# Four low-rank intermediates of the second stream: places of their own, and their stores in GpSimd's queue

## The chip, the cores and the metric

The kernel runs on one core of one Trainium2 chip. The metric is the device time of one launch in microseconds; for the kernel before it is 1659.32 us, the median of three runs (1658.92 to 1660.64). One more execution was taken with the hardware profiler, and every row of the profile comes from that one.

Engine names in the rows: PE is TensorE (matmul), PEld its weight load, DVE is VectorE, ACT is ScalarE, POOL is GpSimd, SPq is the queue of SyncE, which here only issues DMAs. A number such as L591 is a line of the kernel.

## The reference

Two inputs, `x_prompt` and `x_sample`, each 512 tokens by 1024 in fp32, pass through the same two layers with the same weights. The kernel calls them stream 0 and stream 1. Layer 0 is a bidirectional RWKV-7 time mixing, layer 1 a gated neighbourhood attention; the change touches layer 0 only:

```
x_prev, x_next = xn shifted by one token either way
xx = 0.5 * (x_prev + x_next) - xn
lerp(j) = xn + xx * mu[j]
r, k, v = lerp(0) @ w_r, lerp(1) @ w_k, lerp(2) @ w_v ;  z = xn @ w_z
for d in (0, 1):                       # forward and backward scan
    w_log = -softplus(-(w0[d] + tanh(lerp(3+d) @ w1[d]) @ w2[d])) - 0.5
    a     = sigmoid(a0[d] + (lerp(5+d) @ a1[d]) @ a2[d])
    ...                                # decay, scan over 512 tokens, bonus
```

`w1` and `a1` project from 1024 to 64, `w2` and `a2` from 64 back to 1024. So each stream has four low-rank intermediates of 64 x 512: `tanh(lerp(3) @ w1[0])`, `tanh(lerp(4) @ w1[1])`, `lerp(5) @ a1[0]` and `lerp(6) @ a1[1]`. In the kernel they are numbered q = 0 to 3.

## The kernel before

Activations lie transposed, features on the 128 partitions and 512 tokens along the row. A 1024-wide operand is eight tiles of 128 x 512, and an fp32 product is made of three matmuls of a high and a low part: ScalarE casts the high part (L743 for weights, `whi`), VectorE subtracts it for the low part (L745, `wlo`), TensorE multiplies (L824 to L826).

The program has three stages.

The prelude (`prelude(s)`) normalizes each stream, forms the shifted differences, and accumulates the four low-rank projections of all eight tiles in PSUM. At its end, for each pair q2 of intermediates, ScalarE copies a partial sum from PSUM (L581, `lm`), VectorE combines it with its neighbours (L582, L584) and with the other partial sum (L589) into `y`, the first half of a tile `lr`; then ScalarE makes two 64 x 512 intermediates from the halves of `y` (L591, Tanh for q below 2, a copy otherwise). For stream 0 they are split into high and low parts at once and stay in SBUF. For stream 1 they go to DRAM (`save("hid", ...)`, rows `dhid<-lr`) and come back when the scan reaches that stream, near 550 us. The tile `lr` has one buffer. In the kernel before, all four intermediates of a stream are written to the same place, the first 64 partitions of the second half of `lr`.

The scan stage (`scan_phase`) follows. For a pair of heads, `prep` loads `rb` (the inverse norms, from `drn`), `k`, the low-rank weights `w2` and `r` through SyncE's queue in this order; VectorE makes `kk` in the place of `rb` (L876), ScalarE casts the weights' high part `w2h` (L878), VectorE makes the low part `w2l` (L880), ScalarE scales `kk` (L883, `km`), and TensorE multiplies the intermediates with `w2h` and `w2l` (L894, L895). Between these run the columns of the large projections (L824 to L826), with weights loaded in pieces of 128 x 512 through SyncE (`raw`) into three buffers, ScalarE's copies of finished columns (L655) and, where the planner foresees an idle TensorE, filler matmuls (L1641). After a pair's scan, `finish` loads `bv`, `ks`, `sz`; the framework may issue the load of `sz` earlier.

The last stage (`rest`) is the attention layer.

What sets the order: in the scan stage a planner in the kernel (`weave`, with a clock of modelled costs that starts at zero there) writes out the order on TensorE, VectorE and ScalarE by hand. Everything else, the prelude, the last stage and the queues of SyncE and GpSimd throughout, is put in order by the framework from priorities and a modelled timeline of its own, and the tail of the prelude is interleaved with the head of the scan stage. Each queue runs strictly in order on the chip: an instruction that waits holds all behind it.

Memory: the prelude's tiles (`xn`, `lr`, `lm`, `lw`, `xx`, `ls`) lie in a pool that is closed at its end; two pools of the scan stage are opened over the same bytes. A new tile waits for those who still use the old tiles under it, no more. In the kernel before, `rb`, `k`, `r` lie over old `xn` slots; the two `MT` tiles, cleared by GpSimd (L1672), lie over `lr` and `lm` among others; the four slots of `ls`, which the prelude uses for operands and mixed inputs, lie under `ks`, `bv`, `sz` and two small tiles of `finish`.

`save` picks the queue of a store by `store(kind)`: SyncE in the prelude; in the scan stage and later (`self.away`) GpSimd, but for three kinds.

Of the kernel before, what the change touches and what calls it, by code (L numbers as in the profile page):

```python
# [11 lines left out]
F32 = mybir.dt.float32  # L12
# [7 lines left out]
P = 128  # L20
T = 512
# [210 lines left out]
class Trunk:  # L232
# [94 lines left out]
        self.store(kind).dma_start(d, src)  # L327

    def store(self, kind):
        return self.nc.gpsimd if self.away and kind not in ("y", "x1", "h") else self.nc.sync  # L330

    def load(self, dst, src):
        self.nc.sync.dma_start(dst, src)
# [168 lines left out]
    def prelude(self, s):  # L502
        nc = self.nc
        vt, gps, act = nc.vector, nc.gpsimd, nc.scalar
        xs = []
        if s == 0:
            self.vectors()
        for k in range(KT):
            if s == 0 and k == self.WFIRST:
                self.first = [self.weight(self.a["w_z"][0])]  # L510
            t = self.t("xn", (P, T + 2), 16, F32, self.lp)
            self.load(t[:, 1:T + 1], self.a["x"][s][k * P:(k + 1) * P, :])
            xs.append(t)
            if s == 0:

                lo, hi = self.pair()
                act.activation(hi, t[:, 1:T + 1], AF.Identity, scale=self.vec("pre0", k))
                vt.scalar_tensor_tensor(lo, t[:, 1:T + 1], self.vec("pre0", k), hi.bitcast(F32), op0=ALU.mult, op1=ALU.subtract)
                self.xz.append((hi, lo))
                yield  # L520
        if s == 0:
            self.consts()
        acc = self.t("acc") if s else self.t("vs", bufs=self.NVS)
        for k, t in enumerate(xs):
            gps.memset(t[:, 0:1], 0.0)
            gps.memset(t[:, T + 1:T + 2], 0.0)
            self.sumsq(acc, t[:, 1:T + 1], k, vt if s or k % 2 else vt)
            yield
        rstd = self.rstd(acc)
        if s == 0:  # L530
            self.rstd0 = rstd
        yield
        xn, xx = [], []
        for k, t in enumerate(xs):
            x = t[:, 1:T + 1]
            vt.scalar_tensor_tensor(x, x, self.vec("pre0", k), rstd, op0=ALU.mult, op1=ALU.mult)
            xn.append(x)
            yield
        if s == 0:
            yield from self.lora_weights()  # L540
        for k, t in enumerate(xs):
            u = self.t("xx", (P, T), 16, F32, self.lp)
            vt.tensor_tensor(u, t[:, 2:T + 2], t[:, 0:T], op=ALU.add)
            xx.append(u)
            yield
        self.shift[s] = xn, xx

        def mixed(kind, j, k):

            t = self.t("ls", (P, T), 4, F32, self.lp)  # L550
            self.lerp(t, xn[k], xx[k], 8 * j + k)
            self.save("l" + kind, s, k, t)

        pm = self.p("pf", (P, 2, T))
        ps = (self.p("pm"), self.p("us"))
        for k in range(KT):
            if s == 0:
                hi, lo = self.xz[k]
            else:
                hi, lo = (self.t("ls", (P, T), 4, F32R, self.lp) for _ in range(2))  # L560
                self.halves(xn[k], lo, hi, self.alt(k))
            for q2 in range(2):
                for out, w in ((pm[:, q2], self.wm), (ps[q2], self.wl)):
                    a, b = (m[:, k % 4] for m in w[2 * q2 + k // 4])
                    nc.tensor.matmul(out, a, hi, start=(k == 0), stop=False)
                    nc.tensor.matmul(out, a, lo, start=False, stop=False)
                    nc.tensor.matmul(out, b, hi, start=False, stop=(k == KT - 1))
                yield
            for kind, j in (("k", 1), ("r", 0), ("v", 2)) if s else ():
                mixed(kind, j, k)  # L570
                yield
        for q2 in range(2):
            mw = self.t("lm", (P, KT * P), 1, F32, self.lp)[:, 0:T + 2]
            lr = self.t("lr", (P, KT * P), 1, F32, self.lp)
            y, u = lr[:, 0:T], lr[0:64, T:2 * T]
            gps.memset(mw[:, 0:1], 0.0)
            gps.memset(mw[:, T + 1:T + 2], 0.0)
            if s == 0:
                vt.tensor_tensor(mw[:, 1:T + 1], pm[:, q2], rstd, op=ALU.mult)
            else:  # L580
                act.copy(mw[:, 1:T + 1], pm[:, q2])  # L581
            vt.tensor_tensor(y, mw[:, 2:T + 2], mw[:, 0:T], op=ALU.add)  # L582
            yield
            vt.scalar_tensor_tensor(mw[:, 1:T + 1], y, 0.5, mw[:, 1:T + 1], op0=ALU.mult, op1=ALU.subtract)  # L584
            if s == 0:
                vt.tensor_tensor(y, ps[q2], rstd, op=ALU.mult)
                vt.tensor_tensor(y, y, mw[:, 1:T + 1], op=ALU.add)
            else:
                vt.tensor_tensor(y, ps[q2], mw[:, 1:T + 1], op=ALU.add)  # L589
            for q in (2 * q2, 2 * q2 + 1):  # L590
                act.activation(u, y[64 * (q % 2):64 * (q % 2) + 64], AF.Tanh if q < 2 else AF.Copy)  # L591
                if s == 0:
                    self.hidden(q, u)
                else:
                    self.save("hid", s, q, u)
            yield
        if s == 0:
            for k in range(KT):
                mixed("v", 2, k)
                yield  # L600
        if s == 1:
            for k in range(KT):
                self.save("lz", s, k, xn[k])
# [1326 lines left out]
```

## Time and profile before

| | before |
|---|---|
| median of 3 runs | 1659.32 us (1658.92 to 1660.64) |
| the profiled execution | 1659.26 us, span 1657.5 us |
| granted TensorE clock, mean | 0.975 |
| PE busy | 1557.6 us, 94% of the span |
| DVE busy | 1217.3 us, 73% |
| ACT busy | 1013.8 us, 61% |
| POOL busy | 175.8 us, 11% |
| moved by DMA | 336.29 MB, 203 GB/s on average |

How to read the rows that follow. A row of the timeline gives the start in us from the start of the span, the busy time, the engine, the line, the operation, the tile written and the tiles read, a count, and in brackets the idle time of the engine just before it with what ended that. A DMA row on SPq or POOL is the issue alone; the data land later. A row of the waits gives who waited, for whom, the total in us, how often, and the longest. Matmuls overlap, so TensorE's busy time is not its throughput; the distance from one start to the next is the better measure.

### The profile page before, as it was taken

Reading aid. Unit: us, or ns where it says so; the run is one execution under the profiler, and the core shown is the slowest. Engines: PE = TensorE matmul, PEld = TensorE weight load, DVE = VectorE, ACT = ScalarE, POOL = GpSimd, SP = SyncE. Lnnn points to the kernel's source line nnn. Section 1 sums busy time; section 2 is a strip of 40 time slices with the busy share of each in tenths; the row PEclk is TensorE's granted clock in tenths of the full one; section 3 lists DMA queues with packets and bytes.
Section 4 is the critical chain, followed back from the end, with each engine's and each line's share of the span. In section 5 each row is a group of like instructions: output and inputs, shape, how many; then the busy total and the mean of one; then the engine's idle time right before and its main releaser. Section 6 shows DMA issues by size and latency. Waiting matters only on the chain.

```text
span 1657.5 us, 46539 instructions
## 1 busy us (share of the span) xinstructions
PE 1557.6 (94%) x18826; PEld 1197.0 (72%) x18826; DVE 1217.3 (73%) x2711; ACT 1013.8 (61%) x2027; POOL 175.8 (11%) x334
## 2 busy tenths in 40 slices
PE   7989798898999998998988999999999999999998
PEld 6867566776667776776666777777777788777776
DVE  8886469688789787897788897855577585665564
ACT  6567565766755677665575665454567665455562
POOL 0000113311101223010000011000000002100000
PEclk9989899999999999999987999999999999999999
DMA  6455578676687687675776675553765346745553
GB/s 212 154 177 180 163 247 282 211 248 214 228 263 238 209 264 249 207 252 171 243 233 227 201 251 168 178 188 126 265 224 174 109 140 205 246 158 175 171 164 103
DMA packets 176312, 336.29 MB, mean 203 GB/s; under 512 B 20928, under 2 KB 53824, under 8 KB 176096
## 3 DMA queue, kind: packets, MB, share of 16 engines
q1 hardware_dynamic: 152800, 253.60, 48.0%
q0 software_dynamic: 23296, 79.71, 13.6%
q8 instruction: 148, 2.42, 0.6%
q14 instruction: 68, 0.56, 0.1%
HBM read 227.71 MB, written 105.51 MB: 201 GB/s over the span
## 4 chain that ended last, share of the span: by engine, by line
PE 47%; DVE 8%; ACT 5%; DMA 4%; issue 3%; SPq 0%; POOL 0%; DVEq 0%; ACTq 0%; POOLq 0%
PE pg L430 6%; PE pg L431 6%; PE pg L432 6%; PE pm L824 4%; PE pm L825 3%; PE pm L826 3%; PE pf L1112 2%; PE sc L1450 2%; PE po L1483 2%; PE pt L1468 2%; PE us L1231 1%; PE zy L1184 1%; PE us L1211 1%; PE zy L1235 1%; DMA raw<-in_w_in_dram 1%
## 5 line engine op out<-in xcount | busy, mean ns | idle before, releaser
L824 PE MATMUL pm<-act,whi 128*128 128x512 f32 x640 | 285.0, 445 | 8.1 <-ACT act L793 3.2
L825 PE MATMUL pm<-act,whi 128*128 128x512 f32 x640 | 258.0, 403 | 11.7 <-DVE act L771 6.5
L826 PE MATMUL pm<-act,wlo 128*128 128x512 f32 x640 | 256.4, 401 | 5.3 <-DVE wlo L745 5.3
L824 PEld LDWEIGHTS pm<-act,whi 128*128 128x128 f32 x640 | 122.8, 192 | 51.1 <-issue 10.8
L430 PE MATMUL pg<-act,whi 128*128 128x512 f32 x384 | 158.6, 413 | 0.4 <-DVE tmp L1406 0.4
L379 ACT CAST whi<-raw 128x512 fp32r<-128x512 f32 x148 | 91.3, 617 | 106.5 <-PE pg L431 68.7
L431 PE MATMUL pg<-act,whi 128*128 128x512 f32 x384 | 152.6, 397 | 0.0
L432 PE MATMUL pg<-act,wlo 128*128 128x512 f32 x384 | 152.6, 397 | 0.0
L825 PEld LDWEIGHTS pm<-act,whi 128*128 128x128 f32 x640 | 123.5, 193 | 37.9 <-DVE act L771 16.8
L826 PEld LDWEIGHTS pm<-act,wlo 128*128 128x128 f32 x640 | 123.2, 192 | 35.0 <-DVE wlo L745 8.2
L380 DVE TENSOR_TENSOR wlo<-raw,whi 128x512 fp32r<-128x512 f32 x148 | 101.4, 687 | 60.9 <-ACT whi L379 60.2
L745 DVE TENSOR_TENSOR wlo<-raw,whi 128x512 fp32r<-128x512 f32 x160 | 109.1, 684 | 36.4 <-ACT whi L743 36.2
L743 ACT CAST whi<-raw 128x512 fp32r<-128x512 f32 x160 | 97.8, 617 | 42.0 <-PE pm L825 24.3
L430 PEld LDWEIGHTS pg<-act,whi 128*128 128x128 f32 x384 | 72.3, 188 | 15.6 <-issue 3.3
L432 PEld LDWEIGHTS pg<-act,wlo 128*128 128x128 f32 x384 | 72.2, 188 | 14.8 <-issue 0.3
L431 PEld LDWEIGHTS pg<-act,whi 128*128 128x128 f32 x384 | 72.5, 189 | 14.0 <-issue 2.5
L1016 DVE TENSOR_TENSOR etmp<-N 128x30 f32<-128x30 f32 (+14 forms) x240 | 78.6, 328 | 4.3
L1018 DVE TENSOR_TENSOR N<-etmp,N 128x30 f32<-128x30 f32 (+14 forms) x240 | 78.7, 328 | 4.0
L1461 DVE CUSTOM_DVE_ANT_0 sb<-sc,bias 128x256 f32<-128x256 f32 x128 | 49.2, 419 | 27.7 <-PE pt L1468 21.5
L1464 ACT ACTIVATE sb<-sb,mx 128x256 f32<-128x256 f32 x128 | 64.0, 502 | 6.9 <-DVE mx L1463 6.7
L1112 PE MATMUL pf<-cab 64*64 64x128 f32 (+1 forms) x2048 | 66.8, 267 | 0.5 <-issue 0.5
L1135 DVE TENSOR_TENSOR AK<-zy,cc 128x256 f32<-128x256 f32 x63 | 26.6, 422 | 52.0 <-PE zy L1090 51.9
(407 smaller groups left out, 3680.5 us busy)
## 6 DMA issues: line engine op xcount, KB each, us to landing
dab<-ab POOLq DMA_DIRECT2D x32, 1024.0 KB, 7.1
cab<-dab SPq DMA_DIRECT2D x64, 512.0 KB, 4.6
raw<-in_w_in_dram SPq DMA_DIRECT2D x128, 256.0 KB, 3.0
bias<-in_rpb_dram SPq DMA_DIRECT2D x32, 384.0 KB, 5.2
raw<-in_w_z_dram SPq DMA_DIRECT2D x32, 256.0 KB, 3.2
raw<-in_w_k_dram SPq DMA_DIRECT2D x32, 256.0 KB, 3.7
raw<-in_w_r_dram SPq DMA_DIRECT2D x32, 256.0 KB, 3.6
k<-dk SPq DMA_DIRECT2D x32, 256.0 KB, 3.6
```

Source lines behind the costliest of these rows:

```text
L379: self.nc.scalar.copy(hi, src)
L380: (eng or self.nc.vector).tensor_tensor(lo, src, hi.bitcast(F32), op=ALU.subtract)
L430: nc.tensor.matmul(ps, hi, x[k][0], start=(k == 0), stop=False)
L431: nc.tensor.matmul(ps, hi, x[k][1], start=False, stop=False)
L432: self.mm = nc.tensor.matmul(ps, lo, x[k][0], start=False, stop=(k == KT - 1))
L743: nc.scalar.copy(hi, raw[h])
L745: nc.vector.tensor_tensor(lo, raw.pop(h), hi.bitcast(F32), op=ALU.subtract)
L824: nc.tensor.matmul(ps, hi[:, at], xh, start=(k == 0), stop=False)
L825: nc.tensor.matmul(ps, hi[:, at], xl, start=False, stop=False)
L826: nc.tensor.matmul(ps, lo[:, at], xh, start=False, stop=(k == KT - 1))
L1018: vt.tensor_tensor(N[:, q + 1:, :q], tv, N[:, q + 1:, :q], op=ALU.add)
L1112: end = nc.tensor.matmul(st.f[half(a), h, 0, d, g] if st.last else st.f[half(a), h, :, d, g], ab[half(h), d, g, 2 * e[d] + 1 - a], rt if s ...
```

## The change

For stream 1, each of the four intermediates is written to a fresh tile of the tag `ls` (four slots, shared with the prelude's earlier use), instead of the one place in `lr`. The store of each, kind `hid`, is issued from GpSimd's queue instead of SyncE's. Stream 0 is as it was. Nothing else is edited; the arithmetic is the same.

```
     def store(self, kind):
-        return self.nc.gpsimd if self.away and kind not in ("y", "x1", "h") else self.nc.sync
+        return self.nc.gpsimd if kind == "hid" or self.away and kind not in ("y", "x1", "h") else self.nc.sync
...
             for q in (2 * q2, 2 * q2 + 1):
+                if s:
+                    u = self.t("ls", (P, T), 4, F32, self.lp)[0:64]
                 act.activation(u, y[64 * (q % 2):64 * (q % 2) + 64], AF.Tanh if q < 2 else AF.Copy)
                 if s == 0:
                     self.hidden(q, u)
```

More of the change, by code (lines that the diff above doesn't have):

```diff
@@ L329, in store @@
     def store(self, kind):
-        return self.nc.gpsimd if self.away and kind not in ("y", "x1", "h") else self.nc.sync
+        return self.nc.gpsimd if kind == "hid" or self.away and kind not in ("y", "x1", "h") else self.nc.sync
     def load(self, dst, src):
@@ L590, in prelude @@
             for q in (2 * q2, 2 * q2 + 1):
+                if s:
+                    u = self.t("ls", (P, T), 4, F32, self.lp)[0:64]
                 act.activation(u, y[64 * (q % 2):64 * (q % 2) + 64], AF.Tanh if q < 2 else AF.Copy)
```

## The prediction

> **What bounds the kernel now.** I read the page first, for the engine that fills the span, then the windows around the place where the change acts, then the waits, and last the timeline of each queue there. The page says that TensorE is the engine to watch:
>
> ```profile
> PE 1557.6 (94%) x18826; PEld 1197.0 (72%) x18826; DVE 1217.3 (73%) x2711; ACT 1013.8 (61%) x2027; POOL 175.8 (11%) x334
> ```
>
> TensorE's order is fixed in its queue, so an idle stretch in it that shrinks should bring the end nearer, unless a later wait eats the gain. The four intermediates are made near 173 to 186 us. The windows there (each row: the stretch, its length, busy time and count of PE, PEld, DVE, ACT, POOL, the granted clock, DMA share, GB/s):
>
> ```profile
> 170.00:182.00 12.00, 11.82 (x52) 9.16 (x51) 4.26 (x9) 5.15 (x9) 0.79 (x3) 1.00 0.56 159
> 182.00:192.00 10.00, 1.43 (x5) 0.52 (x3) 1.35 (x2) 3.49 (x10) 4.13 (x4) 0.67 0.48 157
> 192.00:200.00 8.00, 8.00 (x28) 6.53 (x29) 6.08 (x9) 5.62 (x10) 0.11 (x1) 0.77 0.16 39
> ```
>
> TensorE is full before 182 and after 192, and nearly empty between: 8.57 us of 10 idle, and every other engine mostly idle as well. This is the largest hole near the change. What ended it (engine, line, waited for: us in total, times, longest):
>
> ```profile
> DVE rb L876 <- DMA k<-dk: 8.8, 1, 8.8
> PE pm L895 <- DVE w2l L880: 4.3, 1, 4.3
> ACT lr L591 <- DMA dhid<-lr: 3.9, 2, 2.0
> ```
>
> TensorE at L895 waits for VectorE's `w2l` (L880), which stands behind `kk` (L876, writing into `rb`), and that waited 8.8 us for the load of `k`. So the question is why `k` came so late. SyncE's own waits and its queue in order of time answer it:
>
> ```profile
> SPq L327 <- ACT lr L591: 2.5, 1, 2.5
> ```
>
> ```profile
> 173.72 0.54 SPq L327 DMA_DIRECT2D dhid<-lr  x1
> 174.34 0.53 SPq L333 DMA_DIRECT2D drn<-tmp  x1
> 176.82 0.47 SPq L327 DMA_DIRECT2D dhid<-lr  x1
> ...
> 178.66 0.33 SPq L333 DMA_DIRECT2D raw<-in_w_r_dram  x1
> 182.12 3.43 SPq L327 DMA_DIRECT2D dhid<-lr  x2
> 185.66 1.18 SPq L333 DMA_DIRECT2D rb<-drn  x2
> 186.89 0.58 SPq L333 DMA_DIRECT2D k<-dk  x1
> ...
> 187.99 0.43 SPq L333 DMA_DIRECT2D sz<-dz  x1
> ...
> 193.18 5.82 SPq L333 DMA_DIRECT2D raw<-in_w_r_dram  x2
> ```
>
> After the weight load at 178.66 SyncE issues nothing until 182.12, is held between the third and the fourth `dhid` store, and only then sends the loads of `rb` and `k`. The inputs of these loads are old: the store `drn` went out at 174.34, `dk` earlier. They wait in line, not for data. ScalarE shows why the stores are late:
>
> ```profile
> 173.59 0.56 ACT L581 COPY lm<-pf 128x512 f32<-128x512 f32 x1
> 176.16 0.63 ACT L591 ACTIVATE lr<-lr 64x512 f32<-64x512 f32 x1 [2.00 <-DMA dhid<-lr]
> 176.70 0.56 ACT L655 COPY tmp<-pm 128x512 f32<-128x512 f32 x1
> 177.29 0.62 ACT L743 CAST whi<-raw 128x512 fp32r<-128x512 f32 x1
> ...
> 182.00 0.56 ACT L655 COPY tmp<-pm 128x512 f32<-128x512 f32 x1
> 184.45 0.63 ACT L591 ACTIVATE lr<-lr 64x512 f32<-64x512 f32 x1 [1.89 <-DMA dhid<-lr]
> 185.10 1.01 ACT L1670 COPY cab<-cc 64x64 f32<-64x64 f32 x4
> 186.13 0.62 ACT L878 CAST w2h<-tmp 128x512 fp32r<-128x512 f32 x1
> ```
>
> Two of the four L591 write a place that the store before them still reads, and wait 2.00 and 1.89 us for it to land.
>
> **The change part by part.** *Own places.* Each L591 of the second stream writes an own slot of `ls`. Both waits go. The second L591 runs behind L581, at about 174.2, 2.0 us earlier. Next on ScalarE is L655, which needs TensorE's first column:
>
> ```profile
> 174.67 0.39 PE L826 MATMUL pm<-act,wlo 128*128 128x512 f32 x1
> 180.86 0.39 PE L826 MATMUL pm<-act,wlo 128*128 128x512 f32 x1
> 181.09 1.46 PE L1641 MATMUL zy<-cc 128*128 128x256 f32 x6
> 186.80 0.80 PE L894 MATMUL pm<-h,w2h 128*128 128x512 f32 x1 [4.26 <-ACT w2h L878]
> 191.91 0.80 PE L895 MATMUL pm<-h,w2l 128*128 128x512 f32 x1 [4.31 <-DVE w2l L880]
> ...
> 194.21 0.63 PE L824 MATMUL pm<-act,whi 128*128 128x512 f32 x1
> ```
>
> That column ends at 174.67 + 0.39 = 175.1, so L655 moves from 176.70 to 175.1, and the cast L743 behind it by the same 1.6 us. VectorE follows:
>
> ```profile
> 177.94 0.69 DVE L745 TENSOR_TENSOR wlo<-raw,whi 128x512 fp32r<-128x512 f32 x1 [5.38 <-ACT whi L743]
> 179.17 0.69 DVE L582 TENSOR_TENSOR lr<-lm 128x512 f32<-128x512 f32 x1 [0.54 <-DMA dhid<-lr]
> ...
> 190.50 0.75 DVE L876 SCALAR_TENSOR_TENSOR rb<-k,cv,rb 128x512 f32<-128x512 f32 x1 [8.85 <-DMA k<-dk]
> 191.17 0.68 DVE L880 TENSOR_TENSOR w2l<-tmp,w2h 128x512 fp32r<-128x512 f32 x1
> ```
>
> L745 goes from 177.94 to about 176.3, and the weight load that it releases on SyncE from 178.66 to about 177.0. L582 no longer waits for a landing (0.54). With L582 at 177 and two more operations of 0.69 us, the third and fourth L591 run at about 179.1 and 179.7 without a gap, where the fourth ran at 184.45.
>
> *GpSimd's queue.* SyncE loses four issues, about 0.5 us each by the two single ones (0.54, 0.47), and with them the hold from 179.0 to 185.6. Its next item is then `rb`. If the weight load in front keeps its time, `rb` goes out at 178.66 + 0.33 = 179.0; if it moves with L745, at 177.4. From the issue of `rb` to the start of L876 the old trace has 190.50 - 185.66 = 4.84 us, with the two `rb` loads, the issue of `k` and its landing in it. So L876 starts between 182.2 and 183.8: a shift of 8.3 to 6.7 us. I take the middle, 7.5, since both ends rest on rows equally near.
>
> Is anything else late next? `w2h` (L878) stands behind the second L655 (182.00) on ScalarE; the four copies at 185.10, 1.01 us together, fall into the idle time ahead of it or behind it. TensorE's second column loses some 0.4 us of stalls, so L655 ends near 182.2 and `w2h` between 182.8 and 183.8: about as early as L876 ends (182.95 to 184.55). With `w2h` at its earliest and `k` no obstacle, L880 would start near 182.8 instead of 191.17: 8.4 us is the most that the shift can be, since TensorE's and ScalarE's own work fills the time up to there. TensorE has its six filler matmuls (1.46) until about 182.2. From L880 on, L895, `km`, the next weight cast and the third column at 194.21 follow at their old distances.
>
> *The clock.* After the hole TensorE is slow: 28 matmuls in 8.00 us (0.286 each) at a granted 0.77, against 52 in 12 us (0.231 each) at 1.00 before it. At the faster pace the 28 need 6.5 us, 1.5 less. The hole in the forecast has two pieces of about 1 to 2 us, in place of two of over 4. I cannot see from here how short a hole must be to leave the clock alone, so the gain lies between 0 and 1.5; I take 1.0, nearer to the upper end because a piece shrinks to less than half. [...]
>
> *What is added.* GpSimd takes four issues. Its queue and the landing of its stores now (the last line is min/median/max of the 64 `dvt` stores):
>
> ```profile
> 182.88 0.54 POOL L327 DMA_DIRECT2D dr<-tmp  x1 [4.64 <-ACT tmp L655]
> 187.48 3.54 POOL L1672 MEMSET MT<- 128x2048 f32 x2 [4.06 <-DMA dhid<-lr]
> ...
> DMA to landing us min/median/max: 2.4/4.7/9.6
> ```
>
> Four times 0.54 is 2.2 us on an engine 11% busy, which was idle 4.64 and 4.06 us before these two items. The memsets wait for the place of `lr`; they may now start near 180.3, so the second `dr` store could stand behind them until 183.9, 1.0 later than now; its reader is the load of `r` for the next preparation. In order behind the waiting `hid` stores stand these `dr` stores and the memsets, nobody that TensorE needs before the third column. The new places are taken over later by `sz`, `bv` and other tiles of the scan's end; the load of `sz` (187.99) is the first. It now waits for a GpSimd store: issued near 180.3, landed by 185.0 at the median, while the weight load behind `sz` would be wanted at 193.18 - 7.5 = 185.7. I cost it at nothing; without that cover (9.6 us landing) it is 189.9, 4.2 us late.
>
> **The sum.** 7.5 + 1.0 = 8.5 us earlier from the third column on. The profiled execution took 1659.26 us (span 1657.5), practically the median of the runs, 1659.32; the forecast is 1650.8. Edges of this case: 6.7 with nothing for the clock gives 1652.6, and 8.4 + 1.5 gives 1649.4.
>
> **The rivals.** *SyncE's order is held anyway, and only issue time is saved.* If the loads of `rb` and `k` hang on the end of the low-rank work and not on the queue, all that SyncE gains is four issues, 2.0 us: 1657.3. For it: the loads are into places of the pool opened behind that work. Against it: the waits list has no wait of those loads, and SyncE goes from `dhid` to `rb` in about 0.1 us. [...]
>
> *The `sz` load holds the weights.* As worked out, a landing of 9.6 us would take 4.2 of the 8.5 back: 1655.0. Against it: the median, and weights already in hand for the third column.
>
> *Slower: a load on SyncE waits for a GpSimd store, ahead of `rb` and `k`.* SyncE's and GpSimd's orders are laid by the framework from a modelled timeline. If it puts `sz` before `rb`, and on GpSimd the last `hid` store behind the memsets and the `dr` store (182.88 + 0.54 + 3.54 = 187.0), the store lands at 187.5 + 4.7 = 192.2, `rb` goes out at 192.7 instead of 185.66, and everything is 7.0 us later: 1666.3. It decides once `rb` is issued after 185.66 + 3.3 = 189.0. Against it: `sz` stands behind `rb`, `k` and `r` today, and ScalarE makes the fourth `hid` before the place of `lr` is free for the memsets.
>
> A different kind of disturbance is the last part, where the framework lays all engines' order anew:
>
> ```profile
> 1000.00:1658.00 658.00, 642.15 (x5794) 502.71 (x5792) 417.24 (x1183) 362.29 (x786) 42.76 (x76) 0.99 0.54 173
> ```
>
> Only 15.9 us of these 658 are idle on TensorE, so there is little to win and a few us to lose; this widens the range and makes no case of its own.
>
> **How the numbers follow.** The forecast has 0.66, its own range 1648.5 to 1653.5. The `sz` rival has 0.09, issue time alone 0.13, slower 0.12. A measurement here tells about 0.2%, 3.3 us, from no change: faster means below 1656.0. Forecast and `sz` make 0.75 faster, issue time 0.13 the same, 0.12 slower. The range must leave out no more than 0.2: from 1647.5, a little below the most that the shift and clock allow, up to 1658.0, which takes in `sz` and the issue-time case and leaves out the slower one.
>
> **What would show it.** Right, if no L591 of the second stream waits for `dhid`; SyncE sends `rb` before 180; L876 starts at 182 to 184 and L895 at 183 to 186; and the stretch up to 200 has the granted clock near 1. Wrong, if SyncE stands still between the weight load and `rb`, if `sz` waits and the weight load behind it comes after 187, or if L895 is early and the end is not: then the gain went into a later wait, to be looked for where TensorE idles before 1000.

## The result, and the profile after

The changed kernel takes 1652.84 us (median of 12 runs, 1647.92 to 1658.72), the kernel before beside it 1659.69 us (12 runs, 1654.07 to 1662.74). The ratio is 0.9967, 95% interval 0.9951 to 0.9982: faster by 5.5 us, between 3.0 and 8.1 (the two medians alone lie 6.9 apart). The profiled execution took 1656.04 us, its span is 1654.2 us; it lies 3 us above the median. Two lines were added, so what was L591 is L593 here, L743 is L745, L876 is L878, L895 is L897, and so on.

The same three stretches as before (columns as there):

```profile
170.00:182.00 12.00, 10.98 (x48) 8.48 (x47) 6.75 (x8) 7.33 (x15) 6.43 (x8) 1.00 0.69 188
182.00:192.00 10.00, 6.69 (x27) 4.42 (x25) 6.02 (x9) 5.61 (x11) 0.67 (x2) 1.00 0.38 135
192.00:200.00 8.00, 7.61 (x93) 6.03 (x94) 4.64 (x7) 6.61 (x15) 1.46 (x2) 1.00 0.69 213
```

Of the 8.57 us that TensorE stood still between 182 and 192, 3.31 are left, and the clock stays at 1.00. SyncE's queue:

```profile
171.32 0.33 SPq L333 DMA_DIRECT2D drn<-tmp  x1
...
178.58 0.33 SPq L333 DMA_DIRECT2D raw<-in_w_r_dram  x1
179.01 1.31 SPq L333 DMA_DIRECT2D rb<-drn  x2
180.37 0.58 SPq L333 DMA_DIRECT2D k<-dk  x1
...
181.53 0.36 SPq L333 DMA_DIRECT2D sz<-dz  x1
187.17 10.59 SPq L333 DMA_DIRECT2D raw<-in_w_r_dram  x4
```

The loads of `rb` and `k` go out at 179.01 and 180.37 instead of 185.66 and 186.89, directly behind the weight load. ScalarE and GpSimd, in order of time:

```profile
171.80 1.28 ACT L593 ACTIVATE ls<-lr 64x512 f32<-64x512 f32 x2
...
175.90 1.28 ACT L593 ACTIVATE ls<-lr 64x512 f32<-64x512 f32 x2 [1.08 <-DVE lr L589]
177.21 0.62 ACT L745 CAST whi<-raw 128x512 fp32r<-128x512 f32 x1
...
181.87 0.62 ACT L880 CAST w2h<-tmp 128x512 fp32r<-128x512 f32 x1
```

```profile
172.73 1.20 POOL L327 DMA_DIRECT2D dhid<-ls  x2 [3.53 <-ACT ls L593]
...
176.83 1.20 POOL L327 DMA_DIRECT2D dhid<-ls  x2 [1.16 <-ACT ls L593]
178.01 3.57 POOL L1674 MEMSET MT<- 128x2048 f32 x2
```

The four L593 come in two pairs, none waits for a landing, and their stores follow within a microsecond. VectorE and TensorE:

```profile
177.86 0.69 DVE L747 TENSOR_TENSOR wlo<-raw,whi 128x512 fp32r<-128x512 f32 x1 [1.99 <-ACT whi L745]
178.47 3.32 DVE L1664 COPY mrx<-cc 128x128 f32<-128x128 f32 x2
184.49 0.75 DVE L878 SCALAR_TENSOR_TENSOR rb<-k,cv,rb 128x512 f32<-128x512 f32 x1 [2.70 <-DMA k<-dk]
185.16 0.69 DVE L882 TENSOR_TENSOR w2l<-tmp,w2h 128x512 fp32r<-128x512 f32 x1
```

```profile
164.53 0.39 PE L567 MATMUL us<-ls,lw 128*128 128x512 f32 x1
...
182.54 0.50 PE L896 MATMUL pm<-h,w2h 128*128 128x512 f32 x1
185.90 0.50 PE L897 MATMUL pm<-h,w2l 128*128 128x512 f32 x1 [2.87 <-DVE w2l L882]
...
187.13 0.39 PE L826 MATMUL pm<-act,whi 128*128 128x512 f32 x1
```

The hole that is left is one wait of 2.87 us at L897, and behind it stands `k` again: VectorE's L878 waited 2.70 us for it.

Two executions differ by up to 2 us before they reach this place (in the nine profiles the last matmul of the prelude starts between 164.53 and 166.41). So below I measure from the last matmul of the prelude (L567, 164.53 here) to the first matmul with `w2l` (L897, 185.90): 21.37 us. In the kernel before:

```profile
165.45 0.39 PE L567 MATMUL us<-ls,lw 128*128 128x512 f32 x1
```

191.91 - 165.45 is 26.46 us, so 5.09 us were won at this place by these two profiles.

### The profile page after: what moved, and what is told of

Same layout as the page of the kernel before. It is cut to its first block, busy times and chain, and to the rows that moved or that the text cites. A ratio compares the mean times of both kernels' runs of the same rounds, so it can differ in the third digit from the quotient of the medians.

```text
span 1654.2 us, 46534 instructions
## 1 busy us (share of the span) xinstructions
PE 1558.4 (94%) x18826; PEld 1195.2 (72%) x18826; DVE 1220.0 (74%) x2711; ACT 1014.5 (61%) x2027; POOL 178.2 (11%) x338
## 4 chain that ended last, share of the span: by engine, by line
PE 48%; DVE 7%; ACT 5%; DMA 3%; issue 3%; POOL 0%; SPq 0%; DVEq 0%; ACTq 0%; POOLq 0%
PE pg L430 6%; PE pg L431 6%; PE pg L432 6%; PE pm L826 4%; PE pm L827 3%; PE pm L828 3%; PE pf L1114 2%; PE sc L1452 2%; PE po L1485 2%; PE pt L1470 2%; PE us L1233 1%; PE zy L1186 1%; PE us L1213 1%; PE zy L1237 1%; DMA v<-dv 1%
## 5 line engine op out<-in xcount | busy, mean ns | idle before, releaser
L747 DVE TENSOR_TENSOR wlo<-raw,whi 128x512 fp32r<-128x512 f32 x160 | 108.9, 683 | 33.3 <-ACT whi L745 33.1
L745 ACT CAST whi<-raw 128x512 fp32r<-128x512 f32 x160 | 97.8, 617 | 44.6 <-PE pm L827 23.3
```

The source lines that it names most:

```text
L745: nc.scalar.copy(hi, raw[h])
L747: nc.vector.tensor_tensor(lo, raw.pop(h), hi.bitcast(F32), op=ALU.subtract)
```

## The experiments

The theory: SyncE was held because ScalarE made the intermediates late, and ScalarE was late because each was written over a place that the store before still read. The rival: what matters is that the stores leave SyncE's queue. A second question was where the lead goes: 6.3 us at 200 us of the span (matching VectorE instructions compared; 0.9 of it was there before this place), 3 us at the end of the first pair of profiles.

**The changed kernel and the kernel before, once more.** No edit.

> The changed kernel once more, unaltered. In its first profile it was about 6 us ahead of the kernel before at 200 us of the span and only 2 to 3 us ahead at 1000 us; the steps back stand at half-clock stretches of TensorE near 474, 546 and 826 us. Theory A (these stretches fall by chance from execution to execution): here the lead at 200 us is again 5 to 6.5 us, the steps back stand elsewhere or are missing, and the lead at the end lies between 2 and 9 us. Rival B (the later order on SyncE's queue, which the framework laid differently, costs the lead): the steps near 474, 546 and 826 us come back at the same places, and the end is again 2 to 3 us ahead in the profile.

> The kernel before once more, for a second profile of it. Theory A of e1: its half-clock stretches after 200 us stand partly at other places than in its first profile (253.9, 294.9, 335.8, 670.3, 762.5, 830.8, 864.9, 895.6, 1202.8 us), and between its two profiles the matching instructions drift by 1 to 4 us. Rival B: the same stretches, and a drift below 1 us. The hole from 182 to 192 us and L895 near 191.9 come back in either case.

The repeated changed kernel has 1654.41 us (median of 12) and a ratio of 0.9966 (0.9947 to 0.9984): the result comes back. Its profiled execution took 1663.56 us, the slowest of its 12, though the program is the same. The places named in the expectation were read some 10 us too late; on the scale of the span they are 464, 536 and 816 us. The windows around the first of them and around a later place, first in the first profile of the changed kernel, then in the second (the last three columns are clock, DMA share and GB/s):

```profile
455.00:475.00 20.00, 16.96 (x383) 12.10 (x377) 14.37 (x33) 11.97 (x26) 1.57 (x3) 0.91 0.73 245
...
1085.00:1100.00 15.00, 13.86 (x365) 10.58 (x364) 9.16 (x14) 8.64 (x17) 0.54 (x1) 1.00 0.55 170
```

```profile
455.00:475.00 20.00, 17.28 (x452) 12.75 (x441) 15.75 (x35) 13.75 (x30) 2.48 (x4) 1.00 0.82 256
...
1085.00:1100.00 15.00, 13.88 (x259) 10.36 (x262) 5.53 (x9) 8.67 (x15) 1.33 (x2) 0.68 0.47 147
```

The slow stretch at 464 (a clock of 0.50 from 465 to 467 us in the first profile) is gone; one at 1090 us is new, and there the second profile falls behind the first by 4.2 us. At 536 and 816 us too the second profile has a clock of 1.00. At 200 us the second profile is 5.1 us ahead of the kernel before, as theory A had it. At the end it is not ahead by 2 to 9 us: the two profiles of one program stand 7.5 us apart, and this one ends behind the first profile of the kernel before. The two profiles of the kernel before drift apart by up to 6 us, more than the 1 to 4 expected, and end 2.6 apart (the second took 1661.88 us); the clock at 810 to 825 us is 0.89 in its first and 1.00 in its second. So theory A holds in that slow stretches move from execution to execution, and rival B's repeated places are refuted. Nor do the many runs show a lead given back: 5.5 us by the times, no less than what the place itself gives below. My bounds for the end of a single profile were too narrow. What the change does is read at its place, and from many runs. There the repeats agree:

```profile
165.34 0.39 PE L567 MATMUL us<-ls,lw 128*128 128x512 f32 x1
...
186.82 0.79 PE L897 MATMUL pm<-h,w2l 128*128 128x512 f32 x1 [3.29 <-DVE w2l L882]
```

```profile
165.72 0.39 PE L567 MATMUL us<-ls,lw 128*128 128x512 f32 x1
...
186.42 0.49 PE L894 MATMUL pm<-h,w2h 128*128 128x512 f32 x1 [4.25 <-ACT w2h L878]
191.45 0.80 PE L895 MATMUL pm<-h,w2l 128*128 128x512 f32 x1 [4.54 <-DVE w2l L880]
```

21.48 us for the changed kernel (21.37 before), 25.73 for the kernel before (26.46). On the means, 21.4 and 26.1, the change wins 4.7 us here.

**Places of their own alone.** Against the changed kernel:

```
-        return self.nc.gpsimd if kind == "hid" or self.away and kind not in ("y", "x1", "h") else self.nc.sync
+        return self.nc.gpsimd if self.away and kind not in ("y", "x1", "h") else self.nc.sync
...
                 if s:
                     u = self.t("ls", (P, T), 4, F32, self.lp)[0:64]
```

> The places of their own alone; the four stores stay in SyncE's queue. Theory A (SyncE was held only because ScalarE made the intermediates late, and ScalarE was late only because it wrote over a place still being stored): the four stores go out between 172 and 178 us without a hold, rb leaves SyncE at 179 to 180, L897 starts at 185 to 187, and the time is that of the full change within 2 us. Rival B (the stores must leave SyncE's queue): rb leaves after 182, L897 starts after 188, and at least half of the gain is gone.

SyncE's queue, VectorE and TensorE:

```profile
173.96 1.17 SPq L327 DMA_DIRECT2D dhid<-ls  x2
...
178.07 1.10 SPq L327 DMA_DIRECT2D dhid<-ls  x2
180.09 0.33 SPq L333 DMA_DIRECT2D raw<-in_w_r_dram  x1
180.53 1.10 SPq L333 DMA_DIRECT2D rb<-drn  x2
```

```profile
185.15 0.75 DVE L878 SCALAR_TENSOR_TENSOR rb<-k,cv,rb 128x512 f32<-128x512 f32 x1 [4.38 <-DMA k<-dk]
```

```profile
166.04 0.39 PE L567 MATMUL us<-ls,lw 128*128 128x512 f32 x1
...
186.56 0.50 PE L897 MATMUL pm<-h,w2l 128*128 128x512 f32 x1 [2.02 <-DVE w2l L882]
```

The time is 1653.87 us (median of 12), ratio 0.9962 (0.9942 to 0.9981); the distance is 20.52 us. `rb` leaves at 180.53, half a microsecond later than expected, but this profile is already 1.5 us behind that of the changed kernel at its L567. Theory A holds: the whole gain is there without GpSimd, and four stores in SyncE's queue cost nothing that shows once they are there in time. At this place the run is even 0.9 us better than the changed kernel (21.4); the times cannot tell the two apart.

**GpSimd's queue alone.** Against the kernel before:

```
+        return self.nc.gpsimd if kind == "hid" or self.away and kind not in ("y", "x1", "h") else self.nc.sync
...
             for q in (2 * q2, 2 * q2 + 1):
                 act.activation(u, y[64 * (q % 2):64 * (q % 2) + 64], AF.Tanh if q < 2 else AF.Copy)
```

> GpSimd's queue alone; all four intermediates are still written to the one place in lr. Theory A (ScalarE's waits are the root): the second and the fourth L591 still wait for a landing, now of a GpSimd store, 2 to 5 us each; rb and k leave SyncE at 179 to 181, so L876 starts near 184.5 as in the full change, but the cast w2h stands behind the fourth L591 and starts at 186 to 188, and L895 starts at 187.5 to 189.5: 2.5 to 4.5 us of the 6 are won. Rival B (only the queue matters): L895 starts near 186 and the whole gain is there.

ScalarE, then SyncE, VectorE and TensorE:

```profile
177.35 0.63 ACT L591 ACTIVATE lr<-lr 64x512 f32<-64x512 f32 x1 [2.49 <-DMA dhid<-lr]
...
187.53 0.63 ACT L591 ACTIVATE lr<-lr 64x512 f32<-64x512 f32 x1 [3.45 <-DMA dhid<-lr]
...
189.21 0.62 ACT L878 CAST w2h<-tmp 128x512 fp32r<-128x512 f32 x1
```

```profile
180.27 1.15 SPq L333 DMA_DIRECT2D rb<-drn  x2
```

```profile
185.76 0.75 DVE L876 SCALAR_TENSOR_TENSOR rb<-k,cv,rb 128x512 f32<-128x512 f32 x1 [2.59 <-DMA k<-dk]
```

```profile
166.34 0.39 PE L567 MATMUL us<-ls,lw 128*128 128x512 f32 x1
...
190.61 0.79 PE L895 MATMUL pm<-h,w2l 128*128 128x512 f32 x1
```

SyncE is free and `rb` leaves early, but ScalarE now waits longer for each landing (2.49 and 3.45 us; 2.00 and 1.89 from SyncE), and `w2h` comes last. The distance is 24.27 us: 1.8 won, less than the 2.5 to 4.5 expected: both waits are at work, the first delays the third L591 (16.64 us after L567, before 16.02), the second the fourth. The time is 1658.29 us (median of 12), ratio 0.9986 (0.9964 to 1.0007), not to be told from no change; its lower edge reaches just past the ratio of the full change, so that the loss of most of the gain is shown by the distance at this place, not by the times. SyncE gained more than the time of the issues: `rb` went out 13.93 us after L567, where it was 20.21, which is 6.3 us earlier, against 2 us for four issues (0.54 and 0.47 us in the two single rows of the kernel before). It won little because ScalarE's waits stayed.

**The weight load out of the way.** What was left ahead of `rb` is the weight load that waits for VectorE. Here this one load goes out from GpSimd's queue; the planner's clock still counts it as SyncE's, so that the order on TensorE, VectorE and ScalarE is that of the changed kernel. Against the changed kernel, the two small edits of the planner's clock left out:

```
-                    raw[2 * c + j] = self.load(self.t("raw", (P, self.WP), self.NRAW), src[:, j * self.WP:(j + 1) * self.WP])
+                    raw[2 * c + j] = dst = self.t("raw", (P, self.WP), self.NRAW)
+                    queue = nc.gpsimd if 2 * c + j == 6 else nc.sync
+                    self.clock.plain(queue.dma_start(dst, src[:, j * self.WP:(j + 1) * self.WP]))
```

> The full change, and the one weight load that stands ahead of rb in SyncE's queue (it waits for the low part of an earlier weight, until 178.6 us) goes out from GpSimd's queue instead. Theory A (what held rb and k from 172 to 179 us after the change was this load, in line ahead of them): rb leaves SyncE at 173 to 175, as soon as drn has landed, k lands before 180, and kk then starts when VectorE is through with the two mrx copies, 181.5 to 183; from the last L567 to the first matmul with w2l it is 19 to 20 us in place of 21.4, and the time is 1 to 2 us below the full change, too little to tell from it. Rival B (rb is held by something else, such as the places it lies over): rb still leaves near 179 and nothing moves.

SyncE, VectorE and TensorE (lines are seven further on than in the changed kernel):

```profile
174.77 1.15 SPq L338 DMA_DIRECT2D rb<-drn  x2
175.97 0.58 SPq L338 DMA_DIRECT2D k<-dk  x1
```

```profile
179.75 0.36 DVE L1671 COPY mrx<-cc 128x128 f32<-128x128 f32 x2
180.73 0.75 DVE L885 SCALAR_TENSOR_TENSOR rb<-k,cv,rb 128x512 f32<-128x512 f32 x1 [0.62 <-DMA k<-dk]
183.80 0.69 DVE L889 TENSOR_TENSOR w2l<-tmp,w2h 128x512 fp32r<-128x512 f32 x1 [2.31 <-ACT w2h L887]
```

```profile
165.96 0.39 PE L572 MATMUL us<-ls,lw 128*128 128x512 f32 x1
...
184.54 0.50 PE L904 MATMUL pm<-h,w2l 128*128 128x512 f32 x1 [0.23 <-DVE w2l L889]
```

`rb` leaves at 174.77 and `kk` starts at 180.73, and VectorE then waits 2.31 us for `w2h`; TensorE waits 0.23 us. The distance is 18.58 us, 2.8 below the changed kernel and a little below the 19 to 20 expected, since the copies were not held (the memsets on GpSimd now stand behind the weight load). Theory A holds: this load was what the loads of `rb` and `k` still stood behind. The time is 1649.41 us (median of 6; the kernel before beside it 1660.83), ratio 0.9933 (0.9912 to 0.9953), the lowest of all; its interval touches that of the changed kernel, so that it beats that one is likely and not shown by this run's times alone. The place accounts for 2.8 us of it; the medians stand 11.4 us below the kernel before, where 7.5 were won here, and no run shows where the rest would come from.

**The same, with the copies on ScalarE.** Further:

```
-            self.nc.vector.tensor_copy(self.mrx[:, d], self.mr[d].unsqueeze(1).broadcast_to([P, 2, L]))
+            self.nc.scalar.copy(self.mrx[:, d], self.mr[d].unsqueeze(1).broadcast_to([P, 2, L]))
```

> As the run before, and the two mrx copies are made by ScalarE instead of VectorE. Theory A (VectorE's copies are held up while GpSimd clears MT, and would now be what kk waits for): kk starts at 179 to 180, the next limit is w2h, which stands behind the second column on ScalarE, so the first matmul with w2l starts 18.3 to 19.2 us after the last L567; time 2 to 3 us below the full change. Rival B (the copies do not matter): the same times as the run before.

```profile
166.41 0.39 PE L572 MATMUL us<-ls,lw 128*128 128x512 f32 x1
...
185.09 0.50 PE L904 MATMUL pm<-h,w2l 128*128 128x512 f32 x1 [0.23 <-DVE w2l L889]
```

18.68 us and 1649.57 us (median of 6; ratio 0.9941, 0.9924 to 0.9957): as the run before. The distance is what theory A gave, but for rival B's reason: the copies were already out of the way, and `w2h` sets the time in both.

**`MT` cleared by VectorE.** Against the changed kernel:

```
         for j in self.MTb:
-            self.nc.gpsimd.memset(j, 0.0)
+            self.nc.vector.memset(j, 0.0)
```

> The full change, with MT cleared by VectorE instead of GpSimd. In the changed kernel the two mrx copies took 3.2 us each in the profile, in place of 0.22 before, and end when GpSimd's two memsets of MT end. Theory A (such a VectorE copy cannot run beside a GpSimd memset): with no memset on GpSimd the copies take 0.2 to 0.3 us each. Rival B (something else made them long): they stay above 1 us. The memsets on VectorE lie in its idle time ahead of kk, so the rest moves by less than 2 us.

VectorE, then TensorE:

```profile
179.93 0.36 DVE L1664 COPY mrx<-cc 128x128 f32<-128x128 f32 x2
```

```profile
186.90 0.79 PE L897 MATMUL pm<-h,w2l 128*128 128x512 f32 x1 [2.37 <-DVE w2l L882]
```

With no memset on GpSimd the two copies take 0.36 us together, against 3.32 in the changed kernel. Theory A holds so far as that GpSimd's memsets made the copies long. The distance is 21.17 us (186.90 from a last L567 at 165.73), so the rest moved by 0.3 us, within the 2 expected; the one execution took 1660.63 us, which tells nothing of the time.

## Why the prediction was right, and where its sizes were off

*Direction and mechanism: right.* No L593 waits for a landing, SyncE's hold is gone, `rb` leaves before 180. I gave no separate share to the two halves of the change; the runs give the gain to the places of their own. GpSimd's queue alone won 1.8 us at this place, and added to the places it won nothing more.

*The shift, 7.5 us (6.7 to 8.3): too large.* From the last L567, 4.7 us were won. In the first pair of profiles `kk` came 25.05 us after L567 before and 19.96 after the change, where the bounds of the forecast amount to 16.75 to 18.35: 1.6 later than the later bound, and at 184.49 outside the 182 to 184 that I had named as a sign. Two parts of the term failed. First, the weight load ahead of `rb`: I took its time as unchanged or 1.6 us earlier, because the cast (L743, here L745) should follow the copy of the finished column at once. The framework put the third and fourth L593 ahead of that cast: ScalarE waited 1.08 us for L589, spent 1.28 us on the two, and made the cast at 177.21. The load went out 14.05 us after L567 where it had been 13.21, so 0.8 later. With that load set aside TensorE gained 2.8 us more, and `w2h` became the limit: only then were 7.5 us won (26.1 - 18.6), by an edit that was not part of the change.

Second, from `rb`'s issue to `kk` I carried over 4.84 us from the kernel before; it took 5.48 (179.01 to 184.49). This time goes with the queue of the stores: 4.84, 4.77 and 4.62 us in the three profiles with the stores in SyncE's queue, 5.03 to 5.96 in the six with them in GpSimd's. Two pairs of these runs differ by the queue alone: 4.62 (places only) against 5.48 and 5.90, and 4.84 and 4.77 (the kernel before) against 5.49. So the second half of the change, for which the prediction counted only GpSimd's issue time and the place of `sz`, cost some 0.9 us here, by these few profiles. Why the loads land later then, no run shows.

*The clock, 1.0 us (0 to 1.5): inside its bounds, but a matter of chance.* From the first matmul with `w2l` to the third column it took 2.30 us in the kernel before (191.91 to 194.21). In the first profile of the changed kernel it was 1.23 (185.90 to 187.13), a gain of 1.1, with the clock between 182 and 200 at 1.00. In the second it was 2.30 again: the first L897 took 0.79 us, and the clock of 182 to 192 was 0.69. The hole of the forecast, two pieces of about 1 to 2 us, was in both one piece, of 2.87 and 3.29 us. A hole of 2.37 us was enough for 0.79 us in the run with `MT` on VectorE, one of 2.87 was not in the first profile. And where L894 took 0.80 us after 4.26 us of idle time in the first profile of the kernel before, it took 0.49 after 4.25 in the second. So the length of the hole alone did not decide it here, and no run shows what did.

*The sum, 8.5 us, against 5.5 (3.0 to 8.1) from the runs:* the shift is too large by 2.8 us, and that is nearly all of the miss. That the forecast of 1650.8 lies only 2 us from the median is in part luck: the medians are 6.9 us apart, more than was won at the place.

*The costs put at nothing* held but for the landing of the loads above: GpSimd's four issues took 2.40 us for the 2.2 worked out, beside other work, and `sz` went out at 181.53 behind `r`. The weight load behind `sz` came at 187.17, past the 187 that I had named as a sign of trouble, but `sz` had not held it: it left right behind the L747 that ended at 187.14 and freed its buffer. The rival of issue time fell with `rb` at 179.01, and its 2.0 us lie below the interval of the runs; the slower rival fell because `sz` stays behind `rb`, `k` and `r`. I had widened the range for the last part, where all orders are laid anew. That reason did not show: the first pair of profiles is 2.2 us apart at 1000 us and 3 at the end. Single executions of one program do differ by more than the change, and that goes with the clock (last section), so the width was right for another reason than the one given.

## What to carry to other kernels

SyncE's queue was a bottleneck here by what waited in it, not by its issue time: without the four stores of about 0.5 us each `rb` left 6.3 us earlier than in the kernel before (GpSimd's queue alone), and without the one weight load of 0.33 us 5.7 us earlier than in the changed kernel (8.81 us after the last matmul of the prelude, where it was 14.48). When a load comes late, look first at what stands ahead of it in its queue and what that waits for. Give a place of its own to a result that is only to be stored, and the hold may go without another queue, as it did here (20.5 us at the place, where it was 26.1); moving the store alone kept the wait on the producer, won 1.8 us at its place and nothing that the times can tell. And where one profile of a kernel differs from the next by more than the effect, read the effect at its place, from a landmark just ahead of it, and the total from many runs.

## What the runs showed of the hardware that was not expected

A VectorE copy of 128 x 128 stretched from 0.22 us to 3.2 us when GpSimd's two memsets of `MT` ran beside it, 178.01 to 181.6, and ended 0.2 us after the second. With `MT` on VectorE, or with the memsets later, the two copies took 0.36 us. With the places alone they started at 179.98, while the first memset was running, and ended some 0.15 us after that one (taken as 1.80 us long, as one memset was with GpSimd's queue alone), before the second was done: 0.79 us together. So they ended just behind one memset or both; by what the two engines held each other up, no run shows. It cost nothing here, since VectorE waited for `k` until 184.49 anyway.

TensorE's half-clock stretches (a granted 0.50, from 465 to 467 us in the first profile of the changed kernel) go with the spread between executions. The same program took 1656.04 and 1663.56 us; at 1085 to 1100 us the clock was 1.00 in one and 0.68 in the other, and 4.2 of the 7.5 us arose there. Among 29 executions of the kernel before, the slowest (1667.80 us) had a mean clock of 0.970, the fastest (1655.25) one of 0.977.
